# Layer 1 of a two-layer decoder trunk: index sums and weight parts moved from VectorE to ScalarE and GpSimd, joint reciprocals, other PSUM banks, later gate projections

## The chip, the cores and the metric

The kernel runs on one core of a Trainium2 chip. The core has TensorE (PE: matmuls, and weight loads, PEld), VectorE (DVE), ScalarE (ACT), GpSimd (POOL) and SyncE (SP, which here only issues transfers). The metric is the device time of one execution in microseconds (us); lower is better. Where several runs are shown, the median counts.

## The reference

The input x has 512 positions of 1024 channels, all in float32. Two layers each add a mixture to the stream. Layer 0 (mLSTM heads and causal pooling) is not touched but for one line of its norm. Layer 1 is:

- xn = rmsnorm(x); one projection of xn gives q (16 heads of 64), a latent ckv (256), four index queries qi of 64, one index key ki of 64, four index weights wi, and a gate z (1024).
- k and v are projections of rmsnorm(ckv); q and k are normalised per head.
- The index score of query t and key s is the sum over the four index heads of `wi * relu(qi . ki)`. For each query the 128 keys with the highest score among those not after it are kept.
- Each head attends to the kept keys with a relative-position bias; softmax, then times v.
- The result times silu(z) is projected by w_out and added to x.

Queries are worked on in four blocks of 128. Block 0 has 128 keys only, so it needs no selection.

## The kernel before

**Products.** Every float32 product is made of three matmuls of a shorter format: each operand is split into a high part and a low part, and high x high, high x low and low x high are summed in PSUM. A weight tile of up to 1024 columns is loaded by a transfer from SP's queue (L146, tile `raw`, three buffers), ACT casts it to the high part (L147, `wh`), and then DVE or POOL subtracts to make the low part (L148, `wl`; three buffers each for `wh` and `wl`). Which of the two engines does so is decided in `run` (L128): it walks through a hand-written order of steps, and a step whose letter is upper case uses DVE, one in lower case POOL. `dense_ch` (L209 to L211 do the matmuls, 512 columns each) projects one block of 128 output channels for all positions; `dense_tok` (L180 to L182) projects token by token.

**Order.** Layer 1's steps stand in the string `ORDER`: `i` are index scores of a block, `C` the latent, `s` a part of the selection (block, part), `q`, `k`, `v`, `z` the projections of a group of four heads (0 to 3), `a` the attention of a group and a block, `y` the split of a finished part for the last projection. From this text a planner builds each engine's queue ahead of time; the order in the text sets priorities, and the planner's own estimate of time decides which ready instruction comes next. On the chip each engine then works in order, and waits for other engines by semaphores.

**Index scores** (`scores`, L704 to L718). For each of blocks 1 to 3 and each of four index heads: PE multiplies, ACT rectifies (L717), and DVE multiplies by wi and adds to the sum `sel` in one instruction (L718). **Selection** (`select`, L720 to L738) takes the eight highest scores at a time on DVE (L725) and replaces them by a mark (L726), four times per part, four parts per block, then turns marks into a mask.

**Attention** (`attend`, L807 to L859) goes through two pairs of heads. For each head POOL adds mask and bias (L826, L829), DVE adds them to the logits and finds the maximum (L832), ACT takes the exponential with its sum (L834), DVE the reciprocal of the sum (L835), ACT scales by it (L836). Then for both heads together PE transposes (L844), ACT and DVE split (L115, L112), PE multiplies by v (L853 to L855), and DVE multiplies by the gate `zy` (L859). The bias of a group of heads comes by a transfer from SP's queue (L786) into one of two buffers.

**Gate.** `z_proj` makes two calls of `dense_ch` per group; DVE scales the result (L803) and ACT takes the SiLU (L804).

**Norm and PSUM.** Between the layers `next_x` adds each output channel block to the stream (DVE, L606), and `squares` sums the squares on POOL (L251); `norm_factors` (L253 to L266) makes the factors from the sum with PE, POOL's power (L260) and DVE. PSUM has eight banks. Layer 0 lays four for `mm` first and then four for `bg`; layer 1 (L621) three for `mm`, two for `qk`, two for `tr`, one for `po`.

Of the kernel before, what the change touches and what calls it, by code (L numbers as in the profile page):

```python
# [53 lines left out]
ORDER = ("i1 i2 C i3 s10 q0 z0 k0 z2 v0 s11 v1 Z1 K1 Q1 s12 s13 s20 s21 s22 a00 Z3 s30 s23 s31 K2 s32 a01 a02 a10 s33 a12 a03 q2 V2 k3 a20 a23 a21 a13 a11 Q3 V3 a22 a33 a31 a32 y32 y31 y0 a30 y33 y30 y1 y2")  # L54
# [3 lines left out]
def trunk(ctx: ExitStack, tc: tile.TileContext, a: dict, out: bass.AP):  # L58
# [10 lines left out]
    def psum_pools(**banks):  # L69
        ps_pools.close()  # L70
        ps.clear()
        for n, b in banks.items():
            ps[n] = ps_pools.enter_context(tc.tile_pool(name="ps_" + n, bufs=b, space=PSUM))

    ctx.callback(ps_pools.close)
    psum_pools(mm=4, bg=4)

    def bank(n):
        return ps[n].tile([128, 512], F32, name=n)
# [164 lines left out]
    def squares(k):  # L244

        if k == 0:
            A.activation(ssum, xT[:, k], AF.Square, scale=1.0 / 32)
            return
        sq = nm.tile([128, S], F32, name="sq", bufs=2)
        A.activation(sq, xT[:, k], AF.Square, scale=1.0 / 32)  # L250
        G.tensor_tensor(ssum, ssum, sq, op=ALU.add)  # L251
# [360 lines left out]
    for c in range(4, NK):  # L612
        dense_ch(y, w_out, 128 * c, lambda ps: next_x(c, ps))
    norm_factors()
# [6 lines left out]
    psum_pools(mm=3, qk=1, tr=2, po=1)  # L621
# [82 lines left out]
    def scores(i):  # L704
# [7 lines left out]
        for h in range(4):  # L712
            if h % 2 == 0:
                pair = next(pairs)
            p = pair[:, h % 2]
            rl = t1.tile([128, 512], F32, name="relu", tag="cb")
            A.activation(rl[:, :n], p[:, :n], AF.Relu)  # L717
            V.scalar_tensor_tensor(acc, rl[:, :n], wi[:, i, h:h + 1], acc, op0=ALU.mult, op1=ALU.add)  # L718
# [88 lines left out]
    def attend(c, i):  # L807
# [8 lines left out]
        for pr, pq in enumerate(pairs):  # L816
            probs = []
            for e in range(2):
# [4 lines left out]
                else:  # L823
                    cb = t1.tile([128, 384], F32, name="cb", tag="cb")
                    if lo:
# [5 lines left out]
                st = t1.tile([128, 4], F32, name="st", bufs=4)  # L831
                V.tensor_tensor_reduce(out=lg[:, :n], in0=p[:, :n], in1=cb[:, :n], scale=-1.0, scalar=3e38,  # L832
                                       op0=ALU.add, op1=ALU.min, accum_out=st[:, 0:1])
                A.activation(lg[:, :n], lg[:, :n], AF.Exp, scale=-1.0, bias=st[:, 0:1], accum_out=st[:, 1:2])  # L834
                V.reciprocal(st[:, 2:3], st[:, 1:2])  # L835
                A.activation(lg[:, :n], lg[:, :n], AF.Copy, scale=st[:, 2:3])  # L836
                probs.append(lg)
            po = bank("po")
# [76 lines left out]
```

## Time and profile before

| | |
|---|---|
| three runs, us | 761.66, 763.02, 762.5 |
| median, us | 762.5 |
| the profiled execution: its own time, us | 760.41 |
| the profiled execution: its span, us | 758.6 |
| granted TensorE clock, mean over the span | 0.997 |

The span runs from the first to the last instruction that the profiler saw; the execution's own time is 1.8 us longer. The profile gives each engine's busy time; matmuls are pipelined and their ends are modelled, so a PE that counts as busy need not be at its peak. POOL's spans are rough. In rows on waits the engine that ended the wait is inferred from semaphores; a wait for several is put down to the one that came last.

### The profile page before, as it was taken

To read this page: it belongs to the slowest core of one execution; us is meant where nothing else is said; L and a number is where in the kernel's file an instruction comes from. 1 tells how busy PE (TensorE), PEld (TensorE's weight loads), DVE (VectorE), ACT (ScalarE), POOL (GpSimd) and SP (SyncE) were. 2 spreads that over 40 slices of the span, in tenths; PEclk is the share of its full clock that TensorE was granted. 3 is DMA by queue.
4 is the path that set the end of the run, shared out by engine and by line. 5 is a ranking of instruction groups with operands and counts; after the bars stand their busy time and mean duration, and the time that the engine had idled before them with its cause. 6 is when DMAs were issued, how large, how long until landed. Compare 5 with 4: busy or idle time off the path is not lost.

```text
span 758.6 us, 11075 instructions
## 1 busy us (share of the span) xinstructions
PE 733.3 (97%) x4123; PEld 621.4 (82%) x4123; DVE 458.2 (60%) x944; ACT 383.8 (51%) x724; POOL 304.2 (40%) x254
## 2 busy tenths in 40 slices
PE   8989999999999999999999999999999998999987
PEld 6887888887888889888988888988898996777776
DVE  6686533434635866235514573399999986788531
ACT  6445333272535544344633453453565775998710
POOL 5455547723002011031363376246234752753321
PEclk9999999999999999999999999999999999999999
DMA  7623342345231323333322143513331220110061
GB/s 223 166 71 86 84 111 70 111 124 153 83 96 59 91 90 88 92 91 93 84 84 84 56 152 114 140 42 88 94 98 57 65 89 29 57 57 1 13 210 55
DMA packets 83989, 69.19 MB, mean 91 GB/s; under 512 B 3884, under 2 KB 71900, under 8 KB 83936
## 3 DMA queue, kind: packets, MB, share of 16 engines
q1 hardware_dynamic: 82144, 65.83, 30.2%
q10 hardware_dynamic: 1760, 2.66, 1.0%
q8 instruction: 32, 0.52, 0.3%
q14 instruction: 21, 0.17, 0.1%
q0 software_dynamic: 32, 0.01, 0.0%
HBM read 64.25 MB, written 4.23 MB: 90 GB/s over the span
## 4 chain that ended last, share of the span: by engine, by line
PE 79%; DVE 12%; ACT 5%; issue 2%; POOL 1%; DMA 1%; SPq 0%; DVEq 0%; POOLq 0%; ACTq 0%
PE mm L209 13%; PE mm L210 13%; PE mm L211 13%; PE mm L180 7%; PE mm L181 7%; PE mm L182 7%; DVE sel L726 1%; ACT lg L834 1%; DVE m L725 1%; DVE sel L718 1%; DVE pt_l L112 1%; PE qk L209 1%; ACT wh L147 1%; PE qk L211 1%; DVE wl L148 1%
## 5 line engine op out<-in xcount | busy, mean ns | idle before, releaser
L148 POOL TENSOR_TENSOR wl<-raw,wh 128x1024 fp32r<-128x1024 f32 (+4 forms) x65 | 148.5, 2285 | 265.0 <-ACT wh L147 220.8
L147 ACT CAST wh<-raw 128x1024 fp32r<-128x1024 f32 (+4 forms) x117 | 113.5, 972 | 175.5 <-PE mm L210 54.4
L209 PE MATMUL mm<-xn_h,wh 128*128 128x512 f32 x336 | 132.5, 396 | 4.4 <-DVE v_l L374 1.9
L210 PE MATMUL mm<-xn_l,wh 128*128 128x512 f32 x336 | 132.3, 394 | 0.0
L211 PE MATMUL mm<-xn_h,wl 128*128 128x512 f32 x336 | 131.9, 392 | 0.0
L182 PE MATMUL mm<-wh,xn_l 128*128 128x256 f32 (+2 forms) x384 | 123.6, 323 | 0.0
L181 PE MATMUL mm<-wl,xn_h 128*128 128x256 f32 (+2 forms) x384 | 123.5, 322 | 0.0
L180 PE MATMUL mm<-wh,xn_h 128*128 128x256 f32 (+2 forms) x384 | 120.8, 323 | 0.9 <-DVE xT L606 0.9
L148 DVE TENSOR_TENSOR wl<-raw,wh 128x1024 fp32r<-128x1024 f32 (+2 forms) x52 | 65.8, 1266 | 63.0 <-ACT wh L147 62.9
L180 PEld LDWEIGHTS mm<-wh,xn_h 128*128 128x128 f32 x384 | 72.0, 188 | 8.3 <-ACT wh L147 1.3
L209 PEld LDWEIGHTS mm<-xn_h,wh 128*128 128x128 f32 x336 | 63.1, 188 | 18.3 <-DVE v_l L374 2.0
L182 PEld LDWEIGHTS mm<-wh,xn_l 128*128 128x128 f32 x384 | 72.2, 188 | 6.4 <-issue 0.6
L181 PEld LDWEIGHTS mm<-wl,xn_h 128*128 128x128 f32 x384 | 72.2, 188 | 6.3 <-issue 0.5
L210 PEld LDWEIGHTS mm<-xn_l,wh 128*128 128x128 f32 x336 | 63.3, 188 | 14.1 <-issue 0.6
L211 PEld LDWEIGHTS mm<-xn_h,wl 128*128 128x128 f32 x336 | 63.2, 188 | 13.9
L211 PE MATMUL mm<-y_h,wl 128*128 128x512 f32 x128 | 50.2, 394 | 0.4 <-DVE wl L148 0.4
L210 PE MATMUL mm<-y_l,wh 128*128 128x512 f32 x128 | 50.3, 393 | 0.0
L209 PE MATMUL mm<-y_h,wh 128*128 128x512 f32 x128 | 48.8, 394 | 0.9 <-ACT y_h L115 0.9
L515 DVE SCALAR_TENSOR_TENSOR cv<-mm,s_conv,cv 128x511 f32<-128x511 f32 (+2 forms) x48 | 35.8, 746 | 16.2 <-ACT cv L513 15.3
L124 POOL TENSOR_TENSOR q_r<-q_ss,mhalf 128x8 f32<-128x8 f32 x16 | 27.2, 1701 | 40.5 <-DVE q_ss L121 32.7
L834 ACT ACTIVATE lg<-lg,st 128x128 f32<-128x128 f32 (+3 forms) x64 | 35.8, 561 | 9.4 <-DVE st L832 9.3
L836 ACT ACTIVATE lg<-lg,st 128x128 f32<-128x128 f32 (+3 forms) x64 | 34.0, 560 | 4.1 <-DVE st L835 3.9
(274 smaller groups left out, 1529.0 us busy)
## 6 DMA issues: line engine op xcount, KB each, us to landing
raw<-in_e_w_in_dram SPq DMA_DIRECT2D x52, 512.0 KB, 3.8
raw<-in_o_w_in_dram SPq DMA_DIRECT2D x18, 512.0 KB, 3.9
raw<-in_e_w_out_dram SPq DMA_DIRECT2D x16, 512.0 KB, 3.7
raw<-in_o_w_out_dram SPq DMA_DIRECT2D x8, 512.0 KB, 3.5
xT<-in_xT_dram SPq DMA_DIRECT2D x8, 256.0 KB, 3.7
x_one<-xT SPq DMA_DIRECT2D x8, 256.0 KB, 2.7
abias<-lines SPq DMA_DIRECT2D x4, 512.0 KB, 3.9
o_sb<-x_one SPq DMA_DIRECT2D x8, 256.0 KB, 4.0
```

The costliest lines, as they stand in the source:

```text
L124: G.tensor_tensor(dst, ss, mhalf[:, :n], op=ALU.pow)
L147: A.copy(wh[:, :n], raw[:, :n])
L148: low_engine[0].tensor_tensor(wl[:, :n], raw[:, :n], wh[:, :n].bitcast(F32), op=ALU.subtract)
L180: T.matmul(ps, ah[:, ts], wh[:, j], start=first, stop=False)
L181: T.matmul(ps, ah[:, ts], wl[:, j], start=False, stop=False)
L182: T.matmul(ps, al[:, ts], wh[:, j], start=False, stop=last)
L209: T.matmul(ps, wh[:, j], ah, start=(k == 0), stop=False)
L210: T.matmul(ps, wh[:, j], al, start=False, stop=False)
L211: T.matmul(ps, wl[:, j], ah, start=False, stop=(k == NK - 1))
L515: V.scalar_tensor_tensor(u[:, j:], ps[:, :S - j], w[:, 3 - j:4 - j], u[:, j:], op0=ALU.mult, op1=ALU.add)
L834: A.activation(lg[:, :n], lg[:, :n], AF.Exp, scale=-1.0, bias=st[:, 0:1], accum_out=st[:, 1:2])
L836: A.activation(lg[:, :n], lg[:, :n], AF.Copy, scale=st[:, 2:3])
```

## The change

1. In `ORDER`, z of heads 4 to 7 goes from before k1 to after selection part s20, and z of heads 12 to 15 from after a00 to just before q3. Five steps change from upper to lower case (z1, k1, q1, k2, v2), so that their weights' low parts are made on POOL; z3, q3 and v3 stay upper case.
2. In `scores`, blocks 2 and 3 scale the rectified scores on ACT and add them on POOL; block 1 stays on DVE. The rectified scores of all blocks go to the six buffers that the logits use later.
3. In `attend`, the two heads of a pair share one tile of statistics and one reciprocal; both scalings follow it.
4. Layer 0's PSUM pools are laid the other way round (`bg` first), and layer 1's pools are opened before `norm_factors`, which so takes its two PSUM tiles from `tr`.
5. The last of the eight square sums is added on DVE, in both layers.

```diff
-ORDER = ("i1 i2 C i3 s10 q0 z0 k0 z2 v0 s11 v1 Z1 K1 Q1 s12 s13 s20 s21 s22 a00 Z3 s30 s23 s31 K2 s32 a01 a02 a10 s33 a12 a03 q2 V2 k3 a20 a23 a21 a13 a11 Q3 V3 a22 a33 a31 a32 y32 y31 y0 a30 y33 y30 y1 y2")
+ORDER = ("i1 i2 C i3 s10 q0 z0 k0 z2 v0 s11 v1 k1 q1 s12 s13 s20 z1 s21 s22 a00 s30 s23 s31 k2 s32 a01 a02 a10 s33 a12 a03 q2 v2 k3 a20 a23 a21 a13 a11 Z3 Q3 V3 a22 a33 a31 a32 y32 y31 y0 a30 y33 y30 y1 y2")
...
-    psum_pools(mm=4, bg=4)
+    psum_pools(bg=4, mm=4)
...
-        G.tensor_tensor(ssum, ssum, sq, op=ALU.add)
+        (V if k == NK - 1 else G).tensor_tensor(ssum, ssum, sq, op=ALU.add)
...
         dense_ch(y, w_out, 128 * c, lambda ps: next_x(c, ps))
+    psum_pools(mm=3, qk=1, tr=2, po=1)
     norm_factors()
...
-    psum_pools(mm=3, qk=1, tr=2, po=1)
...
-            rl = t1.tile([128, 512], F32, name="relu", tag="cb")
+            rl = p2.tile([128, 512], F32, name="relu", tag="lg", bufs=6)
             A.activation(rl[:, :n], p[:, :n], AF.Relu)
-            V.scalar_tensor_tensor(acc, rl[:, :n], wi[:, i, h:h + 1], acc, op0=ALU.mult, op1=ALU.add)
+            if i == 1:
+                V.scalar_tensor_tensor(acc, rl[:, :n], wi[:, i, h:h + 1], acc, op0=ALU.mult, op1=ALU.add)
+            else:
+                A.activation(rl[:, :n], rl[:, :n], AF.Copy, scale=wi[:, i, h:h + 1])
+                G.tensor_tensor(acc, acc, rl[:, :n], op=ALU.add)
...
             probs = []
+            st = t1.tile([128, 6], F32, name="st", bufs=4)
             for e in range(2):
...
-                st = t1.tile([128, 4], F32, name="st", bufs=4)
                 V.tensor_tensor_reduce(out=lg[:, :n], in0=p[:, :n], in1=cb[:, :n], scale=-1.0, scalar=3e38,
-                                       op0=ALU.add, op1=ALU.min, accum_out=st[:, 0:1])
-                A.activation(lg[:, :n], lg[:, :n], AF.Exp, scale=-1.0, bias=st[:, 0:1], accum_out=st[:, 1:2])
-                V.reciprocal(st[:, 2:3], st[:, 1:2])
-                A.activation(lg[:, :n], lg[:, :n], AF.Copy, scale=st[:, 2:3])
+                                       op0=ALU.add, op1=ALU.min, accum_out=st[:, e:e + 1])
+                A.activation(lg[:, :n], lg[:, :n], AF.Exp, scale=-1.0, bias=st[:, e:e + 1], accum_out=st[:, 2 + e:3 + e])
                 probs.append(lg)
+            V.reciprocal(st[:, 4:6], st[:, 2:4])
+            for e in range(2):
+                A.activation(probs[e][:, :n], probs[e][:, :n], AF.Copy, scale=st[:, 4 + e:5 + e])
```

## Rows read from the trace of the kernel before

**Rows 1.** The page's first part: busy us, share of span, count of each engine.
```profile
PE 733.3 (97%) x4123; PEld 621.4 (82%) x4123; DVE 458.2 (60%) x944; ACT 383.8 (51%) x724; POOL 304.2 (40%) x254
```

**Rows 2.** Stretches: length; busy us (count) of PE, PEld, DVE, ACT, POOL; clock.
```profile
80.00:100.00 20.00, 20.00 (x89) 16.41 (x88) 8.84 (x7) 7.24 (x12) 7.02 (x4) 1.00 0.35 93
...
480.00:612.00 132.00, 130.16 (x926) 117.54 (x925) 121.61 (x308) 76.90 (x158) 61.43 (x59) 1.00 0.31 86
492.00:560.00 68.00, 66.16 (x419) 57.39 (x417) 66.49 (x165) 34.27 (x62) 27.91 (x24) 1.00 0.29 78
612.00:722.00 110.00, 100.53 (x709) 83.22 (x708) 82.09 (x265) 86.92 (x213) 52.51 (x68) 0.98 0.13 40
620.00:630.00 10.00, 8.27 (x57) 6.38 (x55) 7.72 (x27) 6.67 (x18) 2.58 (x5) 0.88 0.07 12
```

**Rows 3.** Timeline of PE near 627 us.
```profile
627.44 0.65 PE L679 MATMUL qk<-ak_h,aq_h 64*128 64x512 f32 x1 [1.73 <-DVE st L832]
```

**Rows 4.** Chain of waits, 492 to 612 us: shares of the stretch by line.
```profile
by line: PE mm L180 9.0%; PE mm L181 8.9%; PE mm L182 8.6%; DVE sel L726 8.4%; DVE m L725 7.7%; PE mm L209 7.7%; PE mm L210 7.7%; PE mm L211 7.7%; DVE sel L718 7.1%; PE tr L767 3.1%; DVE q_ss L757 2.6%; DVE q_n L763 2.1%; issue 2.0%; PE qk 
```

**Rows 5.** Groups on DVE, 492 to 612 us: busy us, mean ns, idle before.
```profile
L148 DVE TENSOR_TENSOR wl<-raw,wh 128x1024 fp32r<-128x1024 f32 x7 | 8.5, 1214 | 0.5 <-ACT wh L147 0.5
...
L803 DVE TENSOR_TENSOR zy<-mm,r_bc 128x512 f32<-128x512 f32 x8 | 5.5, 684 | 0.9 <-PE mm L211 0.9
L718 DVE SCALAR_TENSOR_TENSOR sel<-relu,wi,sel 128x512 f32<-128x512 f32 x4 | 4.8, 1206 | 0.0
...
L718 DVE SCALAR_TENSOR_TENSOR sel<-relu,wi,sel 128x384 f32<-128x384 f32 x4 | 4.1, 1025 | 0.0
...
L835 DVE RECIPROCAL st<-st 128x1 f32<-128x1 f32 x14 | 2.0, 152 | 0.7 <-ACT lg L834 0.7
L148 DVE TENSOR_TENSOR wl<-raw,wh 128x512 fp32r<-128x512 f32 x3 | 2.0, 681 | 0.0
```

**Rows 6.** Timeline near 495 us: start, length, engine, line.
```profile
494.30 2.39 POOL L148 TENSOR_TENSOR wl<-raw,wh 128x1024 fp32r<-128x1024 f32 x1 [1.47 <-ACT wh L147]
...
495.50 1.61 DVE L718 SCALAR_TENSOR_TENSOR sel<-relu,wi,sel 128x384 f32<-128x384 f32 x1
...
497.43 0.60 DVE L718 SCALAR_TENSOR_TENSOR sel<-relu,wi,sel 128x384 f32<-128x384 f32 x1
```

**Rows 7.** Groups on ACT, 475 to 758 us.
```profile
L147 ACT CAST wh<-raw 128x1024 fp32r<-128x1024 f32 x26 | 27.3, 1050 | 34.2 <-PE mm L210 9.7 <-DMA out_dram<-o_sb 8.4 <-PE mm L182 6.0
...
L836 ACT ACTIVATE lg<-lg,st 128x512 f32<-128x512 f32 x16 | 10.9, 722 | 1.0 <-DVE st L835 0.9
...
L836 ACT ACTIVATE lg<-lg,st 128x384 f32<-128x384 f32 x16 | 9.3, 610 | 0.0
...
L804 ACT ACTIVATE zy<-zy 128x512 f32<-128x512 f32 x8 | 5.0, 630 | 6.9 <-DVE zy L803 6.8
```

**Rows 8.** Groups on POOL, 475 to 758 us, and last L251, whole span.
```profile
L148 POOL TENSOR_TENSOR wl<-raw,wh 128x1024 fp32r<-128x1024 f32 x16 | 38.5, 2403 | 36.2 <-ACT wh L147 35.0 <-PE qk L211 1.2
L124 POOL TENSOR_TENSOR q_r<-q_ss,mhalf 128x8 f32<-128x8 f32 x16 | 27.2, 1701 | 40.5 <-DVE q_ss L121 32.7 <-DVE q_n L763 7.5 <-PE mm L211 0.2
...
L148 POOL TENSOR_TENSOR wl<-raw,wh 128x512 fp32r<-128x512 f32 x4 | 5.2, 1294 | 2.8 <-ACT wh L147 2.8
...
L251 POOL TENSOR_TENSOR ssum<-ssum,sq 128x512 f32<-128x512 f32 x14 | 22.8, 1632 | 7.9 <-ACT sq L250 7.5
```

**Rows 9.** Waits of SP's queue, 480 to 720 us: total, times, longest.
```profile
SPq L786 <- POOL twin L829: 12.8, 1, 12.8
```

**Rows 10.** Timeline, 464 to 471 us, between the layers.
```profile
464.47 0.39 PE L180 MATMUL mm<-wh,xn_h 128*128 128x324 f32 x1 [0.88 <-DVE xT L606]
...
465.75 1.74 POOL L251 TENSOR_TENSOR ssum<-ssum,sq 128x512 f32<-128x512 f32 x1
...
470.02 0.95 PE L257 MATMUL bg<-ones,ssum 128*128 128x1 f32 x8
```

**Rows 11.** Line L763 on DVE: shortest, median and longest ns, first and last start.
```profile
L763 DVE TENSOR_TENSOR q_n<-mm,q_r x16: 670/680/693, 511.6 to 663.1; 128x512 f32<-128x512 f32 x16
```

## The prediction

> **What bounds the kernel now.** I read the engine totals first: TensorE (PE) counts as busy for 97% of the span [rows 1], so only holes and slow stretches of PE, or PE work that moves into holes, can change the time. Then the busy time by stretch [rows 2]. Layer 0 (the stretch 80 to 100 stands for it) has PE full and VectorE (DVE) half idle: 89 matmuls of 512 columns in 20.00 us, 0.225 us each, and nothing of size is edited there. Layer 1 has two different stages. From 480 to 612 us, the **front** (index scores, selection, nearly all projections), PE is busy 130.2 of 132 us and DVE 121.6 of 132: both are full. From 612 to 722 us, the **tail** (mostly attention, hardly a projection left), PE is busy 100.5 of 110, ScalarE (ACT) 86.9, DVE 82.1: nothing is full and PE starves. Between 620 and 630 PE has 8.27 of 10 us and the granted clock is 0.88, a mixture of the 2.4 and 1.2 GHz levels. It fell after PE had stood for 1.73 us until DVE's logits of block 3 came [rows 3]. The chain of waits in the front alternates between projection matmuls (L180 to L211) and DVE's selection: L726, L725 and the index sums L718 have 8.4%, 7.7% and 7.1% of it [rows 4]. So DVE paces when attention can start, and PE runs its projections meanwhile and has none left for the tail.
>
> **The change, part by part.** Durations are from the profiled execution, 760.4 us (span 758.6); the median of the runs shown is 762.5, 2.1 us above it, and I add those 2.1 at the end.
>
> Index sums of blocks 2 and 3 leave DVE: four of 384 columns, 4.1 us, and four of 512, 4.8 us [rows 5], together 8.9 us. Part of that is collision: one of 384 columns took 0.60 us alone and 1.61 us when it began inside a 2.39 us weight part of GpSimd (POOL) [rows 6]. Against this, ACT gets eight scaled copies, 4 x 0.72 + 4 x 0.61 = 5.3 us by the copies with a scale of L836 [rows 7]; they fit beside ACT's 76.9 of 132 us [rows 2]. POOL gets eight additions: 1.63 us for 512 columns by L251 [rows 8], three quarters of it, 1.2, for 384, in all 11.3 us. POOL worked 27.9 of 68 us from 492 to 560 [rows 2], so I take their cost as nothing. They are covered by block 1's selection on DVE, which the order puts ahead of that of blocks 2 and 3; if POOL is late, selection stops, and that is a rival below. Behind an addition that waits for ACT stand the weight parts and the powers of L124.
>
> Weight parts of z1, k1, q1, k2, v2 go from DVE to POOL: four tiles of 1024 and three of 512 columns, 4 x 1.21 + 3 x 0.68 = 6.9 us off DVE [rows 5], 4 x 2.40 + 3 x 1.29 = 13.5 us on POOL [rows 8]. Three buffers hold split weights, so most of the later arrival (1.2 or 0.6 us a tile, 6.6 us in sum) lies beside matmuls of the tile before: taken as 0, bounds 0 and +6.6.
>
> z3 (heads 12 to 15) moves from the front to just before q3. It is 2 x 24 matmuls of 512 columns, 48 x 0.225 = 10.8 us of PE; two weight casts and two SiLUs, 2 x 1.05 + 2 x 0.63 = 3.4 us on ACT [rows 7]; two weight parts and two products L803, 2 x 1.21 + 2 x 0.68 = 3.8 us on DVE [rows 5]. Its two weight loads now stand in SP's queue behind those of k2, q2, v2 and k3 and behind the bias load of heads 8 to 11. In that queue bias loads stood for up to 12.8 us until bias buffers were free [rows 9], so z3 may come late by that much; I take no loss, since q3 and v3 follow it and would keep PE busy. z1 only moves within the front, past k1's and q1's three loads and a bias load: taken as 0, bounds -1.2 and +1.2, one weight part's length [rows 5].
>
> One reciprocal for two heads: 64 of 152 ns become 32 (mean from [rows 5], where 14 lie in the front), so 7 x 0.152 = 1.1 us less in the front and 25 x 0.152 = 3.8 us in the tail. The price is that head 0's scaling waits for head 1's exponential, up to 0.7 us a pair by the same-sized copy [rows 7]; ACT runs in order and has the next work at hand, so 0, bounds -3.8 and +16 (0.67, the mean of the two sizes in [rows 7], for each of the tail's 24 pairs). The deeper buffers (six for the rectified scores, four per pair for the statistics) only take waits away: 0.
>
> PSUM banks: the first matmul of layer 1 waited 0.88 us for the evacuation of the last output channel (L606). With the mm banks of layer 1 laid where nothing was being evacuated, I take -0.9, bounds -0.9 and 0. The last square sum goes to DVE: the addition was over at 467.5 and its matmul came only at 470.0 [rows 10], so 0; bounds -1.0, and +2.4 behind one POOL weight part [rows 8].
>
> **The sum.** The front loses 8.9 + 6.9 + 3.8 + 1.1 = 20.7 us on DVE and 10.8 us on PE. PE is the tighter, so the front shortens by 10.8. The tail has 9.5 us of PE idle and more in slow matmuls to take z3 in; where ACT and DVE pace it, it lengthens by z3's ACT work, 3.4 (DVE: +3.8 - 3.8, nothing), and the clock dip closes, 10 x 0.12 = -1.2. Total: -10.8 + 3.4 - 1.2 - 0.9 = **-9.5 us**, so 750.9 for such an execution and **753.0** for the median. About 0.2% (1.5 us) is what a measurement can tell from no change.
>
> On collisions, what the trace shows is that DVE operations with two operands in SBUF are the ones stretched by POOL [rows 6], while the 16 products L763, which read PSUM, span 670 to 693 ns whatever POOL did [rows 11]. The Trainium skill, Perfetto Trace Analysis, Optimizing Scalar/DVE Operations, speaks against this change: it says that offloading between VectorE and GpSimd might not help, as they share an SBUF read port. By that rule the time would be that of the shared-port rival below. The Trainium skill, SBUF — State Buffer, Who interferes with whom, narrows it to VectorE instructions with two SBUF inputs (and the two-port modes); by that narrower rule, which these rows bear out, the change removes collisions, as nearly all it leaves in the front reads PSUM or one tensor, and the sum stands.
>
> **The rivals.**
> *GpSimd's queue becomes the path* (slower, 14%). POOL would have 61.4 + 24.8 = 86.2 us in a front of about 121, in order, with the powers (1.7 us, [rows 8]) and mask sums on the same queue. If weights and sums wait there, the front grows by 6.6 us for the slower weight parts and by 11.3 - 8.9 = 2.4 for the sums, and z3's leaving gives nothing because PE is no longer its bound: 760.4 + 9.0 + 2.2 - 0.9 = 770.7, median 772.8. For it: the queue is in order. Against: 41% load from 492 to 560. It decides once POOL is busy over some nine tenths there.
> *The shared port* (slower, 4%). If every added microsecond of POOL also held DVE, DVE would have 121.6 - 20.7 + 24.8 = 125.7 us in the front, at today's filling (121.6 of 132) 136.5 us long: 760.4 + 4.5 + 2.2 - 0.9 = 766.2, median 768.3. The narrow set of stretched operations [rows 6, 11] speaks against it. The Trainium skill's general rule, cited above from Perfetto Trace Analysis, is this case.
> *z3 only moves* (no change, 12%). If the tail is longer by all of z3's 10.8 us, only the banks' 0.9 stay: 759.5, median 761.6. For it: the z3 loads behind the bias load [rows 9]. Against: PE's holes in the tail.
> *DVE was the true bound* (faster still, 13%). Then the front shortens by 20.7, as attention gets into it early: 760.4 - 20.7 + 2.2 - 0.9 = 741.0, median 743.1. PE at 130.2 of 132 speaks against it, the selection's share of the chain for it.
>
> **How the numbers follow.** The forecast has 57%. Faster by over 0.2% gets forecast and last rival, 0.70; same 0.12; slower 0.18. The range 745 to 767 holds the forecast with nearly all of its bounds, the case of no change, and parts of both ends; it leaves out the lower part of the fastest case and most of the POOL case, just under 2 in 10.
>
> **What would show it.** Right: DVE's load in the front falls to about 101 us, while PE stays full and the selection ends some 10 us earlier; no L718 of 1.6 us or more is left; z3's matmuls lie beside attention and the clock holds 1.00 where it was 0.88; the 0.88 us hole before the first layer 1 matmul is gone. Wrong: PE idle that names POOL's wl or index sums, a tail longer by 8 us or more, or exponentials and scalings on ACT further apart than before.

## The result, and the profile after

Four runs took 766.37 to 768.66 us, median **767.56**; four runs of the kernel before beside them took 761.66 to 763.02, median 762.34. The ratio is 1.0072 [1.0056, 1.0087]: the change makes the kernel 0.7% **slower**. The forecast of 753.0 had the wrong sign, and the range (745 to 767) missed by 0.6 us.

The profiled execution of the changed kernel took 768.66 us (span 766.9, 8.3 more than before). First the page's totals, which answer to [rows 1]:

```profile
PE 734.0 (96%) x4123; PEld 621.0 (81%) x4123; DVE 453.1 (59%) x899; ACT 391.4 (51%) x734; POOL 323.5 (42%) x267
```

VectorE (DVE) is busy for 5 us less, GpSimd (POOL) for 19 more, ScalarE (ACT) for 8 more, TensorE (PE) for the same time. The work moved, but VectorE gained little by it: by the rows, operations of some 19 us were to leave it (8.9 + 6.9 + 4.9, less 1.4 for two square sums). The additions of epsilon that stayed on it (L121, tile `q_ss`, 16 in all) grew from 3.5 to 8.1 us; the rest of the difference is not explained here. Then the stretches, with the columns of [rows 2]; the last of them runs to the end of the span:

```profile
480.00:612.00 132.00, 124.81 (x889) 112.49 (x888) 114.16 (x284) 76.04 (x160) 84.55 (x76) 0.97 0.28 77
500.00:520.00 20.00, 17.79 (x108) 15.20 (x108) 19.34 (x55) 9.14 (x16) 16.52 (x13) 0.94 0.27 73
492.00:560.00 68.00, 62.26 (x420) 54.68 (x418) 63.73 (x163) 36.69 (x72) 47.63 (x36) 0.97 0.27 74
612.00:722.00 110.00, 98.96 (x692) 82.03 (x691) 78.30 (x234) 89.12 (x207) 46.31 (x63) 0.98 0.13 40
620.00:630.00 10.00, 10.00 (x58) 7.61 (x58) 6.20 (x20) 8.34 (x17) 1.43 (x2) 1.00 0.23 68
540.00:560.00 20.00, 16.51 (x145) 15.57 (x143) 19.27 (x50) 14.11 (x33) 15.10 (x12) 1.00 0.35 94
560.00:580.00 20.00, 18.55 (x104) 16.71 (x105) 18.13 (x37) 7.63 (x11) 10.03 (x8) 0.91 0.14 39
612.00:766.90 154.90, 138.08 (x875) 113.82 (x873) 89.85 (x257) 97.75 (x221) 58.32 (x68) 0.99 0.19 63
```

The kernel before in three of these stretches:

```profile
540.00:560.00 20.00, 20.00 (x128) 17.60 (x126) 19.46 (x48) 14.00 (x27) 2.31 (x4) 1.00 0.40 105
560.00:580.00 20.00, 20.00 (x152) 18.52 (x151) 19.46 (x47) 10.73 (x19) 10.27 (x8) 1.00 0.28 80
612.00:758.60 146.60, 131.41 (x849) 107.94 (x847) 91.03 (x283) 91.59 (x220) 59.99 (x71) 0.98 0.19 62
```

Read PE's column as a balance. **Front** (480 to 612 us): PE stood still for 132 - 130.16 = 1.84 us before [rows 2] and for 132 - 124.81 = 7.19 after, and its mean clock fell from 1.00 to 0.97 of full speed, which is 0.03 x 132 = 4.0 us more (estimates from the rounded clock, good to about 1 us). **Tail** (612 us to the end): it stood still for 15.2 us before and 16.8 after, although 6.7 us more PE work lies there; the clock rose from 0.98 to 0.99, 1.4 us. The 0.88 us wait ahead of layer 1's first matmul [rows 10] is gone. Together 5.35 + 4.0 + 1.6 - 1.4 - 0.9 = 8.7 us, against the 8.3 of the spans. So the loss is in the front, which was to give the gain, and the tail took z3 in at full price.

What PE waited for, the two rows of the front that matter (engine and line that waited, what ended it; us in total, times, longest):

```profile
PE tr L771 <- DVE q_n L767: 4.7, 1, 4.7
PE mm L209 <- DVE zy L807: 2.2, 1, 2.2
```

So there are two holes. The shorter one ended at 516.8 us; PE had no free `mm` tile there until DVE had scaled a gate projection (L807). It comes back under the experiments. In the longer one PE waited for L771, which transposes a projection that DVE has normalised (L767 of the changed kernel, L763 before). The chain ahead of it is: sum of squares (L761) and addition of epsilon (L121) on DVE, power (L124) on POOL, the product L767 on DVE. The timeline around this hole, as in [rows 6]:

```profile
553.02 2.39 POOL L148 TENSOR_TENSOR wl<-raw,wh 128x1024 fp32r<-128x1024 f32 x1
...
553.63 1.81 DVE L121 TENSOR_SCALAR q_ss<-q_ss 128x8 f32<-128x8 f32 x1
...
555.52 1.65 POOL L124 TENSOR_TENSOR q_r<-q_ss,mhalf 128x8 f32<-128x8 f32 x1
...
557.90 0.66 DVE L121 TENSOR_SCALAR q_ss<-q_ss 128x8 f32<-128x8 f32 x1
...
559.31 0.69 DVE L729 MAX8 m<-sel 128x8 f32<-128x512 f32 x1
...
560.12 0.68 DVE L730 MATCH_REPLACE8 sel<-m,sel 128x512 f32<-128x512 f32 x1
560.71 0.68 DVE L767 TENSOR_TENSOR q_n<-mm,q_r 128x512 f32<-128x512 f32 x1
...
561.45 0.66 PE L771 MATMUL tr<-cst,q_n 128*128 128x128 f32 x4 [4.65 <-DVE q_n L767]
```

Two queues in turn make it late. On POOL a weight part of z1 (moved there by the change, and z1 itself moved behind k1) began at 553.02; the epsilon addition for k1 began 0.6 us later and took 1.81 us instead of 0.15; the power, behind the weight part, ended at 557.17. The product could then have been made, but DVE had four selection steps, the next half's addition and a reciprocal ahead of it in its queue and came to it at 560.71, 3.54 us later. PE had nothing left to do since 556.80, so it stood for 4.65 us. Of these, 0.37 are the wait for the power, 3.54 DVE's queue, and 0.74 the product itself. After the hole the granted clock was 0.91 from 560 to 580 us, and around the shorter one 0.94 from 500 to 520.

The groups on DVE from 492 to 612 us, beside [rows 5]:

```profile
L121 DVE TENSOR_SCALAR q_ss<-q_ss 128x8 f32<-128x8 f32 x12 | 7.2, 600 | 0.1
...
L148 DVE TENSOR_TENSOR wl<-raw,wh 128x1024 fp32r<-128x1024 f32 x3 | 4.2, 1386 | 0.1
L807 DVE TENSOR_TENSOR zy<-mm,r_bc 128x512 f32<-128x512 f32 x6 | 4.1, 681 | 2.1 <-PE mm L211 2.1
...
L840 DVE RECIPROCAL st<-st 128x2 f32<-128x2 f32 x8 | 1.3, 159 | 2.9 <-ACT lg L838 2.9
```

The index sums of blocks 2 and 3 (8.9 us) and the small weight parts are gone, as forecast; a joint reciprocal of two columns takes 159 ns where one of one column took 152.

### The profile page after: what moved, and what is told of

Same layout as the page of the kernel before. It is cut to its first block, busy times and chain, and to the rows that moved or that the text cites. A ratio compares the mean times of both kernels' runs of the same rounds, so it can differ in the third digit from the quotient of the medians.

```text
span 766.9 us, 11056 instructions
## 1 busy us (share of the span) xinstructions
PE 734.0 (96%) x4123; PEld 621.0 (81%) x4123; DVE 453.1 (59%) x899; ACT 391.4 (51%) x734; POOL 323.5 (42%) x267
## 4 chain that ended last, share of the span: by engine, by line
PE 78%; DVE 10%; ACT 6%; issue 2%; POOL 1%; DMA 1%; SPq 1%; ACTq 0%; DVEq 0%
PE mm L209 13%; PE mm L211 13%; PE mm L210 13%; PE mm L180 8%; PE mm L181 8%; PE mm L182 8%; DVE sel L730 1%; ACT lg L838 1%; PE tr L849 1%; PE po L860 1%; DVE m L729 1%; PE qk L682 1%; DVE sq L313 1%; PE qk L209 1%; DMA raw<-in_e_w_in_dram 1%
## 5 line engine op out<-in xcount | busy, mean ns | idle before, releaser
L148 POOL TENSOR_TENSOR wl<-raw,wh 128x1024 fp32r<-128x1024 f32 (+4 forms) x72 | 161.9, 2250 | 275.7 <-ACT wh L147 231.6
L148 DVE TENSOR_TENSOR wl<-raw,wh 128x1024 fp32r<-128x1024 f32 (+2 forms) x45 | 57.1, 1270 | 57.1 <-ACT wh L147 56.7
L838 ACT ACTIVATE lg<-lg,st 128x128 f32<-128x128 f32 (+3 forms) x64 | 35.7, 560 | 10.5 <-DVE st L836 10.3
L124 POOL TENSOR_TENSOR q_r<-q_ss,mhalf 128x8 f32<-128x8 f32 x16 | 27.3, 1707 | 23.3 <-DVE q_n L767 12.5
L842 ACT ACTIVATE lg<-lg,st 128x128 f32<-128x128 f32 (+3 forms) x64 | 32.5, 559 | 3.5 <-DVE st L840 3.5
```

What stands on the lines that cost most here:

```text
L124: G.tensor_tensor(dst, ss, mhalf[:, :n], op=ALU.pow)
L148: low_engine[0].tensor_tensor(wl[:, :n], raw[:, :n], wh[:, :n].bitcast(F32), op=ALU.subtract)
L842: A.activation(probs[e][:, :n], probs[e][:, :n], AF.Copy, scale=st[:, 4 + e:5 + e])
```

## The experiments

Each kernel was timed beside the kernel before on the same chip. Compare kernels by the ratio: the kernel before took 761.2 to 762.4 us, by the median, beside the different kernels. "Wait for q_n" is the longest single wait of PE for a normalised projection, "front idle" 132 us less PE's busy time from 480 to 612, and the clock is that of the same stretch, all three of the profiled execution.

| kernel | median, us | ratio to before | wait for q_n, us | front idle, us | front clock |
|---|---|---|---|---|---|
| before | 762.34 | | 1.1 | 1.84 | 1.00 |
| changed | 767.56 | 1.0072 [1.0056, 1.0087] | 4.7 | 7.19 | 0.97 |
| p1_places | 761.55 | 0.9994 [0.9984, 1.0004] | 2.0 | 5.16 | 1.00 |
| p2_case | 761.82 | 1.0003 [0.9993, 1.0013] | 1.1 | 1.84 | 1.00 |
| p3_sums | 760.74 | 0.9984 [0.9972, 0.9996] | none | 0.00 | 1.00 |
| p4_recip | 762.87 | 1.0011 [1.0000, 1.0021] | 1.1 | 1.84 | 1.00 |
| p5_banks | 765.70 | 1.0053 [1.0040, 1.0066] | 2.9 | 4.50 | 0.99 |
| w2_psum | 766.63 | 1.0068 [1.0055, 1.0081] | 2.9 | 4.50 | 0.99 |
| w3_square | 763.81 | 1.0024 [1.0013, 1.0034] | 2.4 | 4.39 | 0.99 |
| w7_early | 766.69 | 1.0059 [1.0041, 1.0077] | 2.7 | 4.25 | 0.99 |
| u1_places | 759.29 | 0.9978 [0.9966, 0.9991] | none | 2.20 | 1.00 |
| u2_case | 762.08 | 1.0009 [0.9998, 1.0021] | 2.2 | 4.43 | 0.99 |
| u3_sums | 762.03 | 1.0005 [0.9996, 1.0013] | 2.9 | 4.66 | 1.00 |
| w1_nobanks | 762.72 | 1.0009 [0.9999, 1.0020] | 2.5 | 2.50 | 0.99 |
| w5_u1nobanks | 762.79 | 1.0012 [0.9999, 1.0025] | none | 0.00 | 1.00 |
| t1_z1back | 769.01 | 1.0099 [1.0086, 1.0112] | 8.7 | 10.97 | 0.96 |
| t2_z3back | 767.80 | 1.0081 [1.0068, 1.0094] | 4.7 | 7.16 | 0.97 |
| t3_z3cover | 760.51 | 0.9983 [0.9975, 0.9992] | none | 2.24 | 0.99 |
| c1_eps_pool | 768.60 | 1.0087 [1.0072, 1.0102] | 3.6 | 6.07 | 0.97 |
| w4_z1vec | 765.33 | 1.0042 [1.0026, 1.0059] | 1.7 | 4.22 | 1.00 |

**One part alone, on the kernel before.** The places of z1 and z3, their weight parts still on DVE:

```diff
-... v1 Z1 K1 Q1 s12 s13 s20 s21 s22 a00 Z3 s30 ... a11 Q3 ...
+... v1 K1 Q1 s12 s13 s20 Z1 s21 s22 a00 s30 ... a11 Z3 Q3 ...
```

> The kernel before, with only the places of z1 and z3 in the order taken from the change (weight parts stay on VectorE). Theory A (GpSimd: its added work stands ahead of the powers on its queue and holds the small VectorE instructions at the shared port): no change within 2 us, since GpSimd gets nothing. Theory B (cover: z1 no longer stands between v1 and k1, so nothing runs on TensorE while k1 and q1 are normalised): slower by 3 to 6 us, with holes of 2 us or more on TensorE ended by VectorE's q_n (L763) between 540 and 570 us.

No change in time, although the hole that theory B foresaw is there (2.0 us, ended at 559.2). The two halves can be read: in the tail (147.6 us, PE busy 134.95) PE stood for 12.7 us where it stood for 15.2, at a clock of 1.00 where it was 0.98; in the front it stood for 5.2 where it stood for 1.8. So z3 does fill a little of the tail, and the front pays for it.

The weight parts alone, and the index sums of blocks 2 and 3 alone:

```diff
-Z1 K1 Q1 ... K2 ... V2
+z1 k1 q1 ... k2 ... v2
```

> The kernel before, with only the weight parts of z1, k1, q1, k2, v2 on GpSimd. Theory A: slower by 2 to 6 us, with the additions of epsilon (L121) on VectorE stretched from 0.15 to 1 us and more. Theory B: within 1.5 us of the kernel before.

```diff
-            V.scalar_tensor_tensor(acc, rl[:, :n], wi[:, i, h:h + 1], acc, op0=ALU.mult, op1=ALU.add)
+            if i == 1: V.scalar_tensor_tensor(...)
+            else: A.activation(rl, rl, AF.Copy, scale=wi); G.tensor_tensor(acc, acc, rl, op=ALU.add)
```

> The kernel before, with only the index sums of blocks 2 and 3 on ScalarE and GpSimd. Theory A: no gain (within 2 us), as powers and weight parts come later on GpSimd's queue by what VectorE saves. Theory B: faster by 1 to 5 us, as VectorE has 8.9 us less in the stretch where it is full.

Neither loses: 0.0% for 13.5 us more on POOL by the forecast's sum, and 0.2% faster for the sums, with PE never idle in the front. Neither part's load on POOL makes the loss by itself. The joint reciprocal alone:

```diff
-                V.reciprocal(st[:, 2:3], st[:, 1:2])
+            V.reciprocal(st[:, 4:6], st[:, 2:4])
```

> The kernel before, with only the joint reciprocal for two heads. Both theories: within 1.5 us. If the later scaling of the first head costs in the tail (my bound from the copies of L836), slower by 2 to 5 us, with the tail after 612 us longer.

At most 0.2% slower, and that is the edge of the interval. The bank edit with the last square sum, and its pieces:

```diff
-    psum_pools(mm=4, bg=4)
+    psum_pools(bg=4, mm=4)
...
-        G.tensor_tensor(ssum, ssum, sq, op=ALU.add)
+        (V if k == NK - 1 else G).tensor_tensor(ssum, ssum, sq, op=ALU.add)
...
+    psum_pools(mm=3, qk=1, tr=2, po=1)
     norm_factors()
...
-    psum_pools(mm=3, qk=1, tr=2, po=1)
```

> The kernel before, with only the PSUM banks laid otherwise and the last square sum on VectorE. Expected from the 0.88 us wait of the first matmul of layer 1: faster by 0.5 to 1.5 us. If the whole order shifts with it, anything within 2 us.

That was a miss: 3.9 us slower than the runs beside it.

The bank edit without the square sum (w2), the square sum alone (w3), and of the bank edit only the earlier opening of layer 1's pools (w7):

> The kernel before with only the PSUM pools laid as in the changed kernel (square sum on GpSimd as before). Bank theory: the layout shifts the start of layer 1 and the planner's order with it, and costs the 4 us of the joint run, 765 to 767 us. Square theory: the layout gives the 0.9 us of the first matmul's wait and costs nothing, 760.5 to 762 us, and the 4 us come with the square sum on VectorE.

> The kernel before with only the last square sum on VectorE. Bank theory: no change, 761 to 763 us (the prediction's own bounds were -1.0 and +2.4). Square theory: 765 to 767 us, because VectorE does the sum ahead of the first index sums and the order of the front shifts.

> The kernel before with only one half of the bank edit: layer 1's PSUM pools are opened ahead of the norm's factors, so that these take two tiles from tr; layer 0's pools are laid as before. Early-opening theory: this re-deals the planned order of layer 1's first 50 us (the mean squares of q0 come after more index sums) and costs what the whole bank edit costs, 765 to 767.5 us, with a hole of some 3 us on TensorE before the transposes of q0 near 520 us. Layout theory: the swap of mm and bg in layer 0 makes the loss, and this half costs nothing, 760.5 to 762.5 us, without that hole.

This is the one part that costs alone: the banks 5.5 us against the runs beside them; the square sum 2.6 by the medians and 1.8 by the ratio, between its two theories. The earlier opening by itself costs 0.6% where the whole bank edit costs 0.7%, with intervals that overlap, so the swap in layer 0 is not needed for it. It hands the norm's factors two other PSUM tiles, and the order of layer 1 is another one. The timeline of the kernel before for the first half of q0's norm (by its line numbers, in w2 too: L757 sums the squares, L761 multiplies by the norm's factor, L763 is the product q_n):

```profile
504.42 0.84 ACT L755 ACTIVATE q_sq<-mm,r 128x256 f32<-128x256 f32 x2
...
507.65 0.68 DVE L757 TENSOR_REDUCE q_ss<-q_sq 128x8 f32<-128x512 f32 x1
...
509.41 1.64 POOL L124 TENSOR_TENSOR q_r<-q_ss,mhalf 128x8 f32<-128x8 f32 x1 [7.34 <-DVE q_ss L121]
...
511.12 0.30 POOL L761 TENSOR_TENSOR q_r<-q_r,r 128x8 f32<-128x8 f32 x1
```

and that of w2_psum:

```profile
508.54 0.84 ACT L755 ACTIVATE q_sq<-mm,r 128x256 f32<-128x256 f32 x2
...
512.32 0.68 DVE L757 TENSOR_REDUCE q_ss<-q_sq 128x8 f32<-128x512 f32 x1
...
513.48 1.65 POOL L124 TENSOR_TENSOR q_r<-q_ss,mhalf 128x8 f32<-128x8 f32 x1 [0.54 <-DVE q_ss L121]
...
515.09 2.41 POOL L148 TENSOR_TENSOR wl<-raw,wh 128x1024 fp32r<-128x1024 f32 x1
...
517.45 0.20 POOL L761 TENSOR_TENSOR q_r<-q_r,r 128x8 f32<-128x8 f32 x1
...
520.40 0.66 PE L767 MATMUL tr<-cst,q_n 128*128 128x128 f32 x4 [2.95 <-DVE q_n L763]
```

The squares come 4.1 us later, behind index scores on ACT; some 2 us of that are this execution's layer 0, which ended later. Then a weight part of 2.41 us stands on POOL between the power and the product by the factor (L761), where the kernel before has the two next to each other, and DVE's selection steps hold the product q_n for 2 us more. None of the operations shown got slower, and what PE waited for is q_n, not a bank: it is the order. The pattern is that of the changed kernel, without one weight part having changed its engine.

**The changed kernel less one part.** Places of before (u1), weight parts back on DVE (u2), sums back on DVE (u3), and banks and square sum of before (w1):

```diff
-... v1 k1 q1 s12 s13 s20 z1 s21 s22 a00 s30 ... a11 Z3 Q3 ...
+... v1 z1 k1 q1 s12 s13 s20 s21 s22 a00 Z3 s30 ... a11 Q3 ...
```

> The changed kernel with z1 and z3 back at their old places in the order; all else as changed. Alone each part of the change moved the time by no more than 0.2%, so the 5 us come from parts acting together. Theory C (places and GpSimd load together: with z1 behind k1 and q1, TensorE has no other work while k1's normalisation is late on GpSimd and VectorE): back to 758 to 762 us, and the holes of 2.4 and 4.8 us on TensorE before 565 us gone. Theory D (the load on GpSimd and the shared port alone, once sums and weights are both there): stays at 765 us or more.

```diff
-k1 q1 ... z1 ... k2 ... v2
+K1 Q1 ... Z1 ... K2 ... V2
```

> The changed kernel with the weight parts of z1, k1, q1, k2, v2 back on VectorE. Theory C and theory D: back to 758 to 763 us, the stretched additions of epsilon (L121, 7 us of stretch in sum) mostly gone. If instead the places alone cost once VectorE is lighter: stays at 765 us or more.

```diff
-            if i == 1: V.scalar_tensor_tensor(...)
-            else: A.activation(rl, rl, AF.Copy, scale=wi); G.tensor_tensor(acc, acc, rl, op=ALU.add)
+            V.scalar_tensor_tensor(acc, rl[:, :n], wi[:, i, h:h + 1], acc, op0=ALU.mult, op1=ALU.add)
```

> The changed kernel with the index sums of blocks 2 and 3 back on VectorE. Theory D: 759 to 763 us, as GpSimd has 10 us less before 515 us. Theory C: the hole near 515 us goes (q0's powers come earlier), the one near 557 us stays: 763 to 767 us.

```diff
-    psum_pools(bg=4, mm=4)
+    psum_pools(mm=4, bg=4)
...
-        (V if k == NK - 1 else G).tensor_tensor(ssum, ssum, sq, op=ALU.add)
+        G.tensor_tensor(ssum, ssum, sq, op=ALU.add)
...
-    psum_pools(mm=3, qk=1, tr=2, po=1)
     norm_factors()
...
+    psum_pools(mm=3, qk=1, tr=2, po=1)
```

> The changed kernel without its last two parts: PSUM banks laid as before, and the last square sum on GpSimd. The PSUM layout by itself, added to the kernel before, cost 4 us (0.5%); of the parts it alone did. Cover theory (GpSimd's and VectorE's queues deliver a normalised projection late, and TensorE has no projection ahead of its transposes): the parts that make this (order, weight parts, sums) all stay, so the hole of some 4.8 us before a transpose of L771 near 557 us stays and the time is 766 to 769 us. Bank theory (the layout is the 4 us here too, whatever else is changed): 762.5 to 764.5 us, the hole gone or under 2.5 us.

Any one of the four taken out brings the time back to within 0.1% of the kernel before, and the places out to 0.2% below it. These do not add: by the ratios each of them seems to "cost" 0.6% to 0.9%, 2.9% in all, where the whole loss is 0.7%. Two expectations missed. In u3_sums it is the hole near 557 us that shrinks (to 1.2 us) and one of 2.9 us that stays near 518. And w1_nobanks refutes the theory that order, weight parts and sums make the loss by themselves. The stretches of w1_nobanks, front and tail:

```profile
480.00:612.00 132.00, 129.50 (x923) 117.39 (x923) 114.06 (x290) 79.17 (x168) 84.94 (x79) 0.99 0.31 86
...
612.00:761.60 149.60, 134.42 (x870) 111.00 (x868) 89.30 (x253) 97.20 (x221) 58.19 (x68) 1.00 0.19 63
```

POOL is as busy in its front as in the changed kernel (84.9 us) and PE stands for only 2.5 us. Its tail has z3's work and PE is idle for 15.2 us, as before. The longer hole of the changed kernel has shrunk to 2.46 us, and its timeline shows why:

```profile
552.91 2.40 POOL L148 TENSOR_TENSOR wl<-raw,wh 128x1024 fp32r<-128x1024 f32 x1
...
555.43 1.65 POOL L124 TENSOR_TENSOR q_r<-q_ss,mhalf 128x8 f32<-128x8 f32 x1
...
558.45 0.67 DVE L767 TENSOR_TENSOR q_n<-mm,q_r 128x512 f32<-128x512 f32 x1
...
559.17 1.12 PE L771 MATMUL tr<-cst,q_n 128*128 128x128 f32 x4 [2.46 <-DVE q_n L767]
```

The same weight part stands ahead of the same power, which ends at 557.08, again 0.37 us after PE ran dry. But DVE comes to the product 1.37 us after that and not 3.54. The 2.2 us between the two holes are DVE's queue alone. The shorter hole, at 516.8, is not there at all. A wait of 2.2 to 2.4 us for L807 stands at that place in all eight kernels that have both the bank edit and the moved sums, and in none without the bank edit; with the bank edit and the sums on DVE (p5, w2, w7, u3) there is a wait of 2.7 to 2.9 us for q_n between 518 and 520.5.

Then places and banks of before together, with weight parts, sums and reciprocals changed:

```diff
-... z1 k1 q1 ... a00 Z3 ...; bg=4, mm=4; pools before norm_factors; last square sum on V
+... z1 k1 q1 ... a00 Z3 ...; mm=4, bg=4; pools after norm_factors; last square sum on G
```

(the minus side is u1_places.)

> The changed kernel with both gate projections back at their old places, PSUM laid as before and the last square sum on GpSimd: what is left are the weight parts, the index sums and the joint reciprocals. Bank theory with terms that add (taking the banks out of the changed kernel gave 4.9 us, taking the places out 8.3): 753.5 to 756 us, about what the prediction forecast. Order theory (each edit only re-deals one planned order, and the places' gain and the banks' gain are the same hole closed twice): 758.5 to 761.5 us, no better than with the banks changed.

At 762.79 it is slower than either theory said, so the terms do not add, and one hole closed twice is not the whole account. Banks and square sum, which cost the kernel before 0.5% (p5), are worth 0.3% here: 1.0012 without them, 0.9978 with them. PE is not idle at all in w5's front, but a stretch of its tail reads

```profile
620.00:640.00 20.00, 16.66 (x95) 13.66 (x93) 11.88 (x35) 12.84 (x30) 5.14 (x7) 0.74 0.16 53
```

and the same stretch of the kernel before

```profile
620.00:640.00 20.00, 16.38 (x109) 13.24 (x108) 13.76 (x42) 12.99 (x30) 4.84 (x9) 0.91 0.10 28
```

The clock of 0.74 costs 0.26 x 20 = 5.2 us, about the 5.4 by which the profiled span is longer than that of u1_places (762.7 against 757.3). PE had stood for 1.82 us at 627 us, nearly as long as before [rows 3], where the fall cost 0.09 x 20 = 1.8 us. This execution took 764.46 us, 1.7 more than the median of its kernel, and others ran in 761.4, so a part of the 5.2 is this execution's and not the order's.

**Which move makes the hole.** The changed kernel with z1 alone at its old place (t1), z3 alone at its old place (t2), and z3 put where z1 used to stand, with z1 late (t3):

```diff
-... v1 k1 q1 s12 s13 s20 z1 s21 ... a11 Z3 Q3
+... v1 z1 k1 q1 s12 s13 s20 s21 ... a11 Z3 Q3
```

> The changed kernel with z1 alone back between v1 and k1; z3 stays late. Theory E (cover: z1's 48 matmuls are what TensorE does while k1 is normalised): 757 to 761 us, no hole near 557 us, granted clock 1.00 from 540 to 580. Theory F (z3's late place makes the loss, since its work ends in a tail that has no room): 765 us or more.

```diff
-a00 s30 ... a11 Z3 Q3
+a00 Z3 s30 ... a11 Q3
```

> The changed kernel with z3 alone back after a00; z1 stays late. Theory E: 764 to 769 us, with the hole of 4 us or more near 557 us still there. Theory F: 758 to 762 us.

```diff
-... v1 k1 q1 s12 s13 s20 z1 s21 ... a11 Z3 Q3
+... v1 Z3 k1 q1 s12 s13 s20 z1 s21 ... a11 Q3
```

> The changed kernel with z3, not z1, put between v1 and k1; z1 stays at its new place after s20. Theory E: any projection of that length covers k1's normalisation, so 757 to 762 us and no hole near 557 us. If it is z1 that has to be early because its own product is waited for: 765 us or more.

With z1 back the hole at 557 us is gone, as theory E said, but the time it gave is missed by 8 us: one of 8.7 us ends at 584, before the transposes of a later projection. Theory F's number holds, but the wait is in the front and not in the tail. With z3 back the one at 557 stays (4.7). In t1_z1back it is POOL's:

```profile
576.33 2.35 POOL L148 TENSOR_TENSOR wl<-raw,wh 128x1024 fp32r<-128x1024 f32 x1
...
578.63 1.65 POOL L124 TENSOR_TENSOR q_r<-q_ss,mhalf 128x8 f32<-128x8 f32 x1
580.24 1.27 POOL L148 TENSOR_TENSOR wl<-raw,wh 128x512 fp32r<-128x512 f32 x1
...
583.07 0.20 POOL L765 TENSOR_TENSOR q_r<-q_r,r 128x8 f32<-128x8 f32 x1
583.30 1.29 DVE L767 TENSOR_TENSOR q_n<-mm,q_r 128x512 f32<-128x512 f32 x2 [1.77 <-POOL q_r L765]
...
584.14 1.08 PE L771 MATMUL tr<-cst,q_n 128*128 128x128 f32 x4 [8.73 <-DVE q_n L767]
```

Two weight parts, 3.6 us, stand among the powers and ahead of the factors' product. Set the five orders beside each other. A gate projection has no norm, so PE can work on it while a normalised one goes round by DVE and POOL. u1 and t3 have one between v1 and k1 and another between s20 and s30: no wait for q_n, and 0.2% faster than before. The changed kernel and t2 have none in the first place, and wait at 557 us; t1 has none in the second, and waits at 584. Which of z1 and z3 stands there does not matter. The missing projection is what makes a wait possible, not what sets its length: p1_places, u2_case, u3_sums and w1_nobanks have the changed kernel's order too, and wait there for 1.2 to 2.5 us without a loss.

**Which queue.** The epsilon additions of layer 1 on POOL, so that no small DVE operation can be stretched there (c1), and z1's weight parts alone back on DVE (w4):

```diff
-            V.tensor_scalar(ss, ss, more, eps, op0=ALU.add, op1=ALU.add)
+            G.tensor_tensor(ss, ss, more[:, :n], op=ALU.add)
```

> The changed kernel with layer 1's additions of epsilon (L121) made by GpSimd itself, just ahead of its power, so that VectorE has no small instruction there that the shared port can hold. If the 7 us by which these were stretched make the loss: faster than the changed kernel by 3 to 6 us. If the order of work on GpSimd's queue or the places make it: within 1.5 us of the changed kernel, or slower as GpSimd has 18 more instructions.

The stretched additions were real: line L121 on DVE, 490 to 612 us, before and then after (shortest, median, longest ns):

```profile
L121 DVE TENSOR_SCALAR q_ss<-q_ss x12: 151/161/559, 509.2 to 605.5; 128x8 f32<-128x8 f32 x12
```

```profile
L121 DVE TENSOR_SCALAR q_ss<-q_ss x12: 146/412/1811, 510.2 to 601.9; 128x8 f32<-128x8 f32 x12
```

Without them the wait is 3.6 instead of 4.7 us and the time is no better (768.6). They are worth about a microsecond of the hole and do not make the loss.

```diff
-... s20 z1 s21 ...
+... s20 Z1 s21 ...
```

> The changed kernel with the low weight parts of z1 alone back on VectorE; order, sums, reciprocals, banks and all other weight parts as changed. In the changed kernel z1's first part of 2.39 us on GpSimd began at 553.0 and stood ahead of the power of k1's norm (555.5), on which the 4.8 us hole of TensorE hung. Cover theory with GpSimd's queue as its cause: the power begins 2 us or more earlier, the hole shrinks to under 3 us, no or a smaller clock dip follows, and the time falls by 2 to 6 us, to 761.5 to 765.5. Cover theory with VectorE's queue as its cause (the 1.2 us of each weight part and the selection steps come in between there): the hole stays within 1 us and the time within 766 to 769.

The wait falls from 4.7 to 1.7 us and the time by 2.2 us, inside what the theory of POOL's queue gave. But the timeline does not give POOL the whole of it:

```profile
553.78 1.65 POOL L124 TENSOR_TENSOR q_r<-q_ss,mhalf 128x8 f32<-128x8 f32 x1 [1.93 <-DVE q_ss L121]
...
556.74 0.68 DVE L767 TENSOR_TENSOR q_n<-mm,q_r 128x512 f32<-128x512 f32 x1
...
557.48 0.66 PE L771 MATMUL tr<-cst,q_n 128*128 128x128 f32 x4 [1.70 <-DVE q_n L767]
```

PE ran dry at 555.78. The power ended 0.35 us before that, where it had ended 0.37 after: 0.7 us of the gain are POOL's. The product followed 1.31 us after the power, not 3.54: 2.2 us are DVE's queue, which the plan laid out differently, as in w1_nobanks. So taking the weight part away shortens the hole, and most of the shortening comes by another queue. The profiled execution is the fastest of its kernel (762.5, mean clock 0.998) and showed no fall of the clock in the front; three others took 766.0 to 766.1 at a mean clock of 0.990.

## Why the prediction was wrong

**The step that failed first is the sum's largest term, "PE is the tighter, so the front shortens by 10.8", with 3.4 us given back in the tail.** z3 did leave the front. But PE's work in all is the same (733.3 and 734.0 us), so it is no gain unless it fills idle time later, and PE's idle time in the tail, 15.2 us, is 15.2 in w1_nobanks and 16.8 in the changed kernel, with z3 in it. The forecast read 9.5 us of idle PE time in the tail as room. It is not room in one piece: most of it is waits of under 2 us each in attention, and z3, placed ahead of q3, runs before most of them (its matmuls lie between 611 and 628 us in the changed kernel). This is the rival "z3 only moves". It was given 12%, and without the bank edit it is what happened: 762.72, against the 762.5 that the rival gives without the banks' 0.9. p1_places shows how far the forecast was right: with the places alone, 2.5 us of tail idle were filled and its clock rose to 1.00, and the front lost 3.3 us of PE time.

**The term "z1 only moves within the front", taken as 0 with bounds -1.2 and +1.2, priced its loads and not what PE does meanwhile.** z1's matmuls were the work that PE had while k1 was normalised. A gate projection put back in that place, with another still between s20 and s30, takes the ratio from 1.0072 to 0.9983 (t3_z3cover); z1 put back with none left there only moves the wait to 584 us (t1_z1back).

**The step with the wrong sign is the bank term, -0.9 with bounds -0.9 and 0.** The 0.88 us was gained exactly as read in [rows 10]. The bounds priced one wait and left out that the edit changes the planner's input. Alone it costs 0.7%, and taken out of the changed kernel together with the square sum it gives 0.6% back: the hole at 516.8 goes, and the one at 557 shrinks by 2.2 us. The square sum, put at 0 with bounds -1.0 and +2.4, was mis-sized too: +2.6 us by the medians, with a wait of 2.4 us for q_n that ended at 569.8.

**"I take their cost as nothing" (sums on POOL) and "taken as 0, bounds 0 and +6.6" (weight parts)** hold for each part alone, by p3 and p2. They fail together with the new places and the banks. The document's own warning, "behind an addition that waits for ACT stand the weight parts and the powers of L124", named POOL's half of the chain; what it did not price is a power behind a weight part, nor the product behind DVE's selection steps. The rival "GpSimd's queue becomes the path" had the right sign and one of the two queues, and the wrong point: it was to decide at nine tenths of POOL's time. POOL was busy for 70% from 492 to 560 us (47.63 of 68), and w1_nobanks loses nothing with the same load (49.36 of 68) and with the same weight part ahead of the same power. What decides is the order on both queues between PE's last matmul and the product, and in the traces set side by side above (changed kernel, w1_nobanks, w4_z1vec) DVE's part is the larger: 2.2 us, against 0.7 of POOL's.

**The port.** The shared-port rival was 768.3 and the result 767.6, which is chance: it needs DVE busy for 125.7 us in the front, and DVE was busy for 114.2; and c1 takes DVE's stretched additions away and the time stays. But the narrow reading in the prediction was too narrow. It went by operations with two operands in SBUF [rows 6], and L121 has one and was stretched from 0.15 to 1.81 us. The Trainium skill, SBUF — State Buffer, Who interferes with whom, also lists `tensor_scalar` among the operations that can take the port shared with GpSimd; the trace agrees, the 1.81 us addition having begun at 553.63 inside the weight part of 553.02 to 555.41 and ended with it.

**Right** were: PE as the front's bound rather than DVE. w5_u1nobanks has 10.6 us less DVE work from 480 to 612 and PE never idle, and is no faster for it. And the selection, which was to end some 10 us earlier, ends 20 us earlier in the changed kernel, and no time comes of it, so the rival "DVE was the true bound" does not hold. Its last step, a copy of the mask, before and then after (shortest, median, longest ns, first and last start):

```profile
L738 POOL COPY twin<-sel x1: 402/402/402, 602.4 to 602.4; 128x256 f32<-128x256 f32 x1
```

```profile
L742 POOL COPY twin<-sel x1: 396/396/396, 582.6 to 582.6; 128x256 f32<-128x256 f32 x1
```

Right were also the collisions of L718, which are gone; the first matmul's wait; the clock of 1.00 from 620 to 630 us; the joint reciprocal at about nothing (its upper bound counts 24 pairs in the tail where its saving counts 25; nothing hangs on that). The clock term, -1.2, came true in the tail (-1.4); the 4.0 us of slower clock in the front had no term. DVE's load in the front came down to 114.2 us and not to 101. The first sign named for "wrong", PE idle that names POOL, came in another form: the wait names DVE's q_n, and POOL's share of it only shows when its chain is followed back. "A tail longer by 8 us or more" came as written: 154.9 against 146.6.

**In one sentence:** the edits each re-deal one planned order; as combined, PE twice has nothing left to do in the front, for 2.2 us at 516.8 and for 4.65 at 557, the second time because a power stands behind a weight part on POOL and, for longer, its product behind selection steps on DVE, and the holes and the slower clock after them cost more than anything that the edits saved. What stays open is why the planner puts them there: its estimates of time are not in the trace. Open too is when a hole lowers the clock. The same wait of 2.2 us for L807 stood beside a clock of 0.94 from 500 to 520 us in the changed kernel (first group of stretches) and of 1.00 in u1_places:

```profile
500.00:520.00 20.00, 17.80 (x115) 15.39 (x114) 19.31 (x56) 9.43 (x17) 16.81 (x14) 1.00 0.25 68
```

and in w5_u1nobanks the clock fell beside a wait of 1.8 us at 627 and cost 5 us.

u1_places has the lowest ratio: 759.29 us, 0.9978 [0.9966, 0.9991] of the kernel before, though t3_z3cover and p3_sums lie within its interval. It is the change without its new places.

## What to carry to other kernels

Where a planner lays out in-order queues, an edit's price is not the price of its operations: plan the changed kernel and see which instructions stand ahead of each short operation that TensorE will wait for, on every engine of its chain, before summing any durations. Idle time of TensorE is room for moved work only if the work can be cut into pieces as small as the holes and stand beside them; here most of it only moved. Time the parts both ways, alone and left out: parts that each seem to cost the whole loss when left out, and nothing when alone, are one order and not a sum.

## What was not expected of the hardware

A VectorE addition on 8 columns with one operand in SBUF took 1.81 us inside a GpSimd weight part, twelve times its 0.15. And executions of one program differ by the granted clock: w4_z1vec ran in 762.5 us at a mean clock of 0.998, and in 766.1 at 0.990. Where the clock fell in the longer ones no trace shows.
